# A hybrid attention trunk: difference heads divided by their sums as a row, and a short feed-forward with gate operands made step by step and up-projection in 512 columns

## The chip, the cores and the metric

The kernel runs on one core of a Trainium2 chip. The metric is the device time of one execution in microseconds (us), the median of several runs; lower is better. The core has five engines with instruction queues of their own: TensorE (PE, matrix products; its weight loads are shown apart as PEld), VectorE (DVE), ScalarE (ACT), GpSimd (POOL) and SyncE (SP, which here only issues transfers). Products land in PSUM, other tiles lie in SBUF, and transfers to and from memory run beside all engines.

## The reference, cut to what matters

One layer is applied to two sequences with shared weights: a long one of 1024 positions and a short one of 512, each with 16 learned positions ahead of it. D_MODEL is 1024, a head has 64 columns, D_FF is 2816.

```python
n = rms_norm(x, g_mix);  qa, ka, va, qb, kb, vb = split(n @ w_in)
# group A: 8 query heads over 2 key heads, softmax, times va
# group B: 4 difference heads, each with two softmax maps
s = einsum('bqhcd,bkhcd->bhcqk', qblk, kb) * scale
p = softmax(s, axis=-1)
a = p[:, :, 0] - lam * p[:, :, 1]
ob = einsum('bhqk,bkhe->bqhe', a, vb)
ob = rms_norm(ob, g_subln) * (1.0 - lam_init)
x = x + concat([oa, ob]) @ w_out

n = rms_norm(x, g_ffn);  gate = n @ w_ff_gate
gate = pad[:, :-2]*conv_w[0] + pad[:, 1:-1]*conv_w[1] + pad[:, 2:]*conv_w[2] + conv_b
x = x + (gelu(gate) * (n @ w_ff_up)) @ w_ff_down
```

A last rms_norm follows, and the 16 positions are dropped. Where rms_norm is taken of a difference head, a common factor of a query's 128 values cancels but for the 1e-6 that is added to their mean square.

## The kernel before, in words

Products are kept near float32: an operand is split into a rounded high part (a cast on ACT, L114) and a low part (a subtraction, L115, on DVE or POOL), and a product is three matmuls, high by high, high by low, low by high (`mm3`, L121 to L123). `dense` (L126) does this for eight blocks of 128 rows, 24 matmuls into one PSUM bank. Weights come as a whole tile w_f by SP's queue and are split in SBUF (`load_weight`, L171).

The stages, with the time at which they run in the profiled execution: the projection of the short sequence (to about 150 us); the short attention beside the long projection (to about 510); the long attention (`attention`, L383) beside the short sequence's output projection and feed-forward (`conv_glu`, L748), to about 1325; the long output projection, beside the rest of the short feed-forward (to about 1450); the long feed-forward in two layers of a seven-product scheme on half blocks (to the end). Two parts that run beside each other are generators that `merge` (L1234) advances in a given ratio of the costs that they yield. This gives the order in which instructions are written down. A planner with a model of the engines then sets each engine's own order and hands out buffers: what is written down first goes first, and where it isn't ready by the model, something later takes its place. On the chip each engine keeps the order that was set.

A difference head (`diff_block`, L523) takes a block of queries in two or three columns of tiles (102 to 114 queries each): three blocks for each of the 4 long heads, two for each of the 4 short heads, 20 blocks in all with 56 columns. For each column `softmax` (L424) makes scores (L431, L432), moves them from PSUM with their maximum (L433, L436), and takes Exp with the sum over keys in `l` (L438). Nothing is divided: p0 stays as it is, and p1 is scaled by c = -lambda * l0 / l1 (L531) and added (L532), so that the result is l0 times the wanted difference. `weighted_v` (L445) transposes it block of keys by block of keys (L456), splits it (pt_hi, pt_lo) and multiplies it by the values into the PSUM tile "o" (L466 to L468), of which there is one; L480 is the last, for the remaining keys. Then ACT copies o (L541) and squares it (L543), one matmul with ones_v takes the mean square into "o" again (L545), and `rsqrt_newton` (L98) makes the factor for L551. Since o is l0 times too large, the 1e-6 has to be l0 squared times as large: for each column ACT makes a tile e, the square of l0 times a constant (L535), and a matmul of e by the diagonal matrix eps_d adds it to the mean square (L548).

The short feed-forward takes the 22 blocks of D_FF in groups of two. For each block there are two chunks of 256 positions (`centres`, L768): gate with 258 columns and its convolution (L782 to L787), GELU over the group (L790), then up, multiplied by the gate (L802) and split, the low part a_lo on POOL (L803); then `down` (L808) for eight blocks of columns at 512 positions, added to h on DVE (L814). Between the weights of the group that begins with block 12 and its `down`, `presplit` (L868) makes four sums and differences of quarters of the first two gate weight tiles, splits them and stores them in memory for the long feed-forward (L884 to L894). Its subtractions run on DVE, and it has two steps.

## Time and profile before

| | |
|---|---|
| median of 3 runs | 2126.57 us (2126.3 to 2130.99) |
| profiled execution | 2138.1 us, its span 2136.3 us |
| granted TensorE clock, mean | 0.982 |
| chain that ended last | PE 76%, DVE 12%, DMA 4%, ACT 3%, issue 3% |
| HBM read, written | 211.13 MB, 82.85 MB |
| transfers, mean busy share of the 16 engines (hardware queue) | 41.6% |

A profile is one execution as the hardware profiler took it, on one core. Matmuls are pipelined: a row shows when one started and a modelled end, and neighbours overlap, so that the distance from start to start is the price of one in a row of them. "Idle before, releaser" is the time that an engine stood still ahead of a group and whose signal ended it. A group's line number can be that of a helper; then the tile names tell it apart. In the stretches, each engine's busy time and its count of instructions stand in the order PE, PEld, DVE, ACT, POOL, then the granted clock, the share of the transfer engines and GB/s. The lists of waits give the waiting instruction, the one that it waited for, the us in total, how often, and the longest.

### The profile page before, as it was taken

What the parts mean: (1) busy time and instruction counts of PE and PEld (TensorE: products, weight loads), DVE (VectorE), ACT (ScalarE), POOL (GpSimd) and SP (SyncE); (2) the same over time, 40 slices, a digit from 0 to 9 for tenths busy, and PEclk for the clock granted to TensorE, in tenths of its full rate; (3) what the DMA queues carried; (4) which work ended last, traced back from release to release, by engine and by line L of the source; (5) the groups of instructions that cost most, each with busy time, mean ns of one, the idle gap of its engine ahead of it and who ended that gap; (6) DMA issues with size and microseconds to landing.
All of it is one profiled execution on the core that took longest, in us unless ns stands there. A gap on an engine that the chain in (4) does not pass through costs nothing.

```text
span 2136.3 us, 35264 instructions
## 1 busy us (share of the span) xinstructions
PE 2051.1 (96%) x12302; PEld 1833.1 (86%) x12302; DVE 1724.1 (81%) x3786; ACT 1156.8 (54%) x2253; POOL 582.7 (27%) x534
## 2 busy tenths in 40 slices
PE   6999999999999999999999999979999999999998
PEld 6988888997887999899989999978888777778877
DVE  6878889767879788888988885578878878869886
ACT  6635566544657556666666765345444444435454
POOL 4653233553112000000000000542444444330112
PEclk8999999999999999999999999998999999999999
DMA  7564335456621322223352224986232232247443
GB/s 252 178 198 133 118 110 170 153 182 226 206 84 55 105 75 70 70 85 114 103 188 77 93 88 145 300 256 229 101 109 89 97 115 84 94 166 258 119 126 126
DMA packets 164897, 296.30 MB, mean 139 GB/s; under 512 B 21456, under 2 KB 82672, under 8 KB 164208
## 3 DMA queue, kind: packets, MB, share of 16 engines
q1 hardware_dynamic: 162416, 287.76, 41.6%
q0 software_dynamic: 2304, 6.29, 0.8%
q8 instruction: 97, 1.59, 0.3%
q14 instruction: 80, 0.66, 0.1%
HBM read 211.13 MB, written 82.85 MB: 138 GB/s over the span
## 4 chain that ended last, share of the span: by engine, by line
PE 76%; DVE 12%; DMA 4%; ACT 3%; issue 3%; POOL 1%; SPq 1%; DVEq 0%; ACTq 0%; POOLq 0%
PE ps_mm L121 17%; PE ps_mm L123 17%; PE ps_mm L122 17%; PE ps_t L456 5%; PE ps_s L431 3%; PE ps_s L432 3%; PE ps_s L121 2%; PE ps_s L122 2%; PE ps_s L123 2%; PE ps_o L471 2%; PE ps_o L470 2%; DVE p L433 1%; DVE w_lo L115 1%; DMA m<-oT 1%; DVE acc L979 1%
## 5 line engine op out<-in xcount | busy, mean ns | idle before, releaser
L121 PE MATMUL ps_mm<-xhi,w_hi 128*128 128x258 f32 (+3 forms) x1264 | 383.4, 304 | 12.0 <-ACT xhi L114 3.7
L122 PE MATMUL ps_mm<-xlo,w_hi 128*128 128x258 f32 (+3 forms) x1264 | 379.0, 300 | 0.3 <-POOL xlo L115 0.3
L123 PE MATMUL ps_mm<-xhi,w_lo 128*128 128x258 f32 (+3 forms) x1264 | 377.2, 299 | 0.3 <-DVE w_lo L115 0.3
L433 DVE TENSOR_SCALAR_CACHE_REDUCE p<-ps_s 114x344 f32<-114x344 f32 (+4 forms) x562 | 257.6, 488 | 30.2 <-PE ps_s L432 19.1
L114 ACT CAST pt_hi<-ps_t 128x512 fp32r<-128x512 f32 (+6 forms) x360 | 169.3, 483 | 181.0 <-PE ps_t L456 155.2
L121 PEld LDWEIGHTS ps_mm<-xhi,w_hi 128*128 128x128 f32 x1264 | 240.0, 190 | 17.5 <-ACT xhi L114 5.4
L438 ACT ACTIVATE p<-p,nm 114x1040 f32<-114x1040 f32 (+5 forms) x212 | 214.8, 1013 | 72.8 <-DVE nm L436 71.8
L115 DVE TENSOR_TENSOR w_lo<-w_f,w_hi 128x1024 fp32r<-128x1024 f32 (+1 forms) x182 | 192.8, 1067 | 66.2 <-ACT w_hi L114 65.6
L122 PEld LDWEIGHTS ps_mm<-xlo,w_hi 128*128 128x128 f32 x1264 | 240.3, 190 | 1.9 <-POOL xlo L115 0.7
L123 PEld LDWEIGHTS ps_mm<-xhi,w_lo 128*128 128x128 f32 x1264 | 240.0, 190 | 1.2 <-DVE w_lo L115 0.5
L114 ACT CAST w_hi<-w_f 128x1024 fp32r<-128x1024 f32 (+1 forms) x199 | 167.6, 856 | 84.9 <-PE ps_mm L122 57.5
L115 DVE TENSOR_TENSOR pt_lo<-ps_t,pt_hi 128x512 fp32r<-128x512 f32 (+4 forms) x312 | 171.7, 561 | 43.7 <-ACT pt_hi L114 42.3
L115 POOL TENSOR_TENSOR a_lo<-gate,a_hi 128x256 fp32r<-128x256 f32 x44 | 43.3, 985 | 545.3 <-ACT a_hi L114 525.9
L431 PE MATMUL ps_s<-k,q 128*114 128x348 f32 (+4 forms) x552 | 183.6, 338 | 3.4 <-DVE p L433 3.2
L456 PE MATMUL ps_t<-ident,p 128*128 128x128 f32 (+7 forms) x1188 | 183.0, 270 | 1.0 <-DVE nm L436 0.5
L432 PE MATMUL ps_s<-k,q 128*114 128x348 f32 (+4 forms) x552 | 171.1, 315 | 0.0
L121 PE MATMUL ps_s<-xhi,w_hi 128*128 128x256 f32 (+4 forms) x480 | 148.7, 313 | 20.4 <-ACT xhi L234 8.2
L456 PEld LDWEIGHTS ps_t<-ident,p 128*128 128x128 f32 (+7 forms) x1188 | 140.4, 136 | 29.6 <-issue 6.8
L123 PE MATMUL ps_s<-xhi,w_lo 128*128 128x256 f32 (+4 forms) x480 | 147.4, 307 | 1.4 <-DMA w_lo<-wo 1.4
L122 PE MATMUL ps_s<-xlo,w_hi 128*128 128x256 f32 (+4 forms) x480 | 148.6, 310 | 0.0
L121 PE MATMUL ps_mm<-t_hi,w_hi 128*128 128x512 f32 (+2 forms) x368 | 144.6, 393 | 1.2 <-DVE v L934 1.2
L123 PE MATMUL ps_mm<-t_hi,w_lo 128*128 128x512 f32 (+2 forms) x368 | 144.4, 392 | 0.1
(275 smaller groups left out, 5309.4 us busy)
## 6 DMA issues: line engine op xcount, KB each, us to landing
w_f<-w_gate SPq DMA_DIRECT2D x46, 512.0 KB, 3.5
w_f<-w_up SPq DMA_DIRECT2D x44, 512.0 KB, 3.4
w_f<-w_in SPq DMA_DIRECT2D x36, 512.0 KB, 3.9
a_f<-act SPq DMA_DIRECT2D x62, 256.0 KB, 2.7
w_f<-w_down SPq DMA_DIRECT2D x22, 512.0 KB, 3.3
act<-a_t SPq DMA_DIRECT2D x44, 256.0 KB, 2.1
a<-w_down SPq DMA_DIRECT2D x40, 256.0 KB, 5.4
w_hi<-wo SPq DMA_DIRECT2D x36, 256.0 KB, 5.1
```

The lines of the kernel that those rows point to most:

```text
L114: return (nc.scalar.copy(hi, src).ins, (lo_engine or nc.vector).tensor_tensor(out=lo, in0=src, in1=hi.bitcast(F32), op=ALU.subtract).ins)
L115: (lo_engine or nc.vector).tensor_tensor(out=lo, in0=src, in1=hi.bitcast(F32), op=ALU.subtract).ins)
L121: nc.tensor.matmul(ps, lhsT=whi, rhs=xhi, start=start, stop=False)
L122: nc.tensor.matmul(ps, lhsT=whi, rhs=xlo, start=False, stop=False)
L123: return nc.tensor.matmul(ps, lhsT=wlo, rhs=xhi, start=False, stop=stop).ins
L431: nc.tensor.matmul(ps, lhsT=q[0], rhs=k[:, c0:c0 + cw], start=True, stop=False)
L432: nc.tensor.matmul(ps, lhsT=q[1], rhs=k[:, c0:c0 + cw], start=False, stop=True)
L433: nc.vector.tensor_scalar(out=p[:, c0:c0 + cw], in0=ps, scalar1=HD ** -0.5, scalar2=-3.0e38, op0=ALU.mult, op1=ALU.max, accum_out=mx[:, i: ...
L438: g.last_exp = nc.scalar.activation(p, p, AF.Exp, bias=nm, accum_out=l).ins
L456: nc.tensor.transpose(tps[:, c:c + M], p[:, k0:k0 + kw], g.ident[:M, :M])
L470: nc.tensor.matmul(o, lhsT=v[:, i, :], rhs=hi, start=i == 0, stop=False)
L471: nc.tensor.matmul(o, lhsT=v[:, i, :], rhs=lo, start=False, stop=False)
```

## The change

In the difference heads the sums l0 of a block's columns are written next to each other into one tile of four columns. After the first block of keys of `weighted_v`, DVE takes their reciprocal, PE transposes it into a "t" tile of PSUM, ACT copies it to SBUF and issues from its own queue a transfer of it to a row in memory. After the second block of keys, SP issues a transfer that reads the row into all 128 partitions (the tile `r_rows`, one buffer). When the values are done, ACT copies o as before, POOL multiplies the copy by the row, and ACT squares that. The tiles e, the matrix eps_d and their matmuls are gone, and the 1e-6 is added in `rsqrt_newton` as elsewhere.

In the feed-forward of the short sequence up runs over 512 positions at once; gate remains at two chunks. `presplit` is advanced by one step after each of the eight column blocks of `down`, its steps are six, its subtractions and its sum run on POOL, and the quarter tiles are kept in the order 1, 2, 0, 3.

```diff
-    def softmax(q, k, inverse=True):
+    def softmax(q, k, inverse=True, l=None):
...
-        l = sp.tile([P, 1], F32, name="l", tag="l")[:M]
+        if l is None:
+            l = sp.tile([P, 1], F32, name="l", tag="l")[:M]
...
+    rows = op.tile([P, 512], F32, name="r_rows", tag="r_rows", bufs=1)
...
-    def diff_block(qs, ks, v, cols):
-        pl, el = [], []
-        for c0, M in cols:
-            p0, l0, _ = softmax([x[:, c0:c0 + M] for x in qs[0]], ks[0], False)
+    def diff_block(qs, ks, v, cols, row):
+        nt, M, W = len(cols), cols[0][1], sum(m for _, m in cols)
+        pl = []
+        l0 = sp.tile([P, 4], F32, name="l0", tag="l0", bufs=2)[:M, :nt]
+        for i, (c0, _) in enumerate(cols):
+            p0 = softmax([x[:, c0:c0 + M] for x in qs[0]], ks[0], False, l0[:, i:i + 1])[0]
             p1, _, r1 = softmax([x[:, c0:c0 + M] for x in qs[1]], ks[1])
...
-            e = op.tile([P, P], F32, name="e", tag="e", bufs=6)[:M]
-            nc.scalar.activation(e, g.ones_d[:M], AF.Square, scale=l0)
-            el.append(e)
             pl.append(p0)
             yield 4 * n
-        o, W = yield from weighted_v(pl, v, True)
+        value = weighted_v(pl, v, True)
+        yield next(value)
+        nc.vector.reciprocal(out=l0, in_=l0)
+        ps = g.psum.tile(nt, M, "t")
+        nc.tensor.transpose(ps, l0, g.ident[:M, :M])
+        lt = sp.tile([4, P], F32, name="lt", tag="lt", bufs=1)[:nt, :M]
+        nc.scalar.copy(lt, ps)
+        nc.scalar.dma_start(out=row[:W].rearrange("(t p) -> t p", p=M), in_=lt)
+        yield next(value)
+        nc.sync.dma_start(out=rows[:, :W], in_=row[:W].unsqueeze(0).broadcast_to([P, W]))
+        o, W = yield from value
         ob = op.tile([P, 512], F32, name="o_b", tag="o")[:, :W]
         nc.scalar.copy(ob, o)
+        nc.gpsimd.tensor_tensor(out=ob, in0=ob, in1=rows[:, :W], op=ALU.mult)
...
-        nc.tensor.matmul(ms, lhsT=g.ones_v, rhs=sq, start=True, stop=False)
-        for e, (c0, M) in zip(el, cols):
-            c = c0 - cols[0][0]
-            nc.tensor.matmul(ms[:, c:c + M], lhsT=e, rhs=g.eps_d[:M, :M], start=False, stop=e is el[-1])
+        nc.tensor.matmul(ms, lhsT=g.ones_v, rhs=sq, start=True, stop=True)
...
-        rsqrt_newton(g, op, rs, ms, W, 0.0)
+        rsqrt_newton(g, op, rs, ms, W)
...
-            for c0, cw in centres:
+            for c0, cw in even_chunks(N, 512):
                 up = g.psum.tile(P, cw, "mm")
...
-        if f0 == FPRE:
-            yield from presplit(g, wp, ap)
         if grp[-1] < NFF - 1:
+            pre = presplit(g, wp, ap) if f0 == FPRE else iter(())
             for j in range(KT):
                 for c0, cw in even_chunks(N, 512):
                     down(j, c0, cw)
                     yield 3 * len(grp) * cw
+                next(pre, None)
+            drain(pre)
             continue
...
     def minus(out, a, b):
-        nc.vector.tensor_tensor(out=out, in0=a, in1=b, op=ALU.subtract)
-
-    kept(0, raw[0])
+        nc.gpsimd.tensor_tensor(out=out, in0=a, in1=b, op=ALU.subtract)
+
     t = ap.tile([P, 2, H], F32, name="gate", tag="gate", bufs=1)
-    nc.vector.tensor_tensor(out=t[:, 0], in0=a21, in1=a22, op=ALU.add)
+    nc.gpsimd.tensor_tensor(out=t[:, 0], in0=a21, in1=a22, op=ALU.add)
     minus(t[:, 1], t[:, 0], a11)
+    yield
     kept(1, t.rearrange("p x c -> p (x c)"))
-    yield 0
+    yield
 
     minus(t[:, 1], a12, t[:, 1])
     minus(t[:, 0], a11, a21)
+    yield
     kept(2, t.rearrange("p x c -> p (x c)"))
+    yield
+    kept(0, raw[0])
+    yield
     kept(3, a22, H)
-    yield 0
```

The remaining edits give the function's callers the row (`g.r`, twelve rows in memory for each sequence) and take eps_d out of the constants.

More of the change, by code (lines that the diff above doesn't have):

```diff
@@ L561, in attention @@
         v = load_v(1 + h, 2 * P, 0)
-        rows = g.oT[s][512 + h * P:512 + (h + 1) * P]
+        out = g.oT[s][512 + h * P:512 + (h + 1) * P]
         for blk in blocks:
@@ L566, in attention @@
             qs = [load_q(QB + h, m, c0, W) for m in range(2)]
-            ob = yield from diff_block(qs, ks, v, [(c - c0, m) for c, m in blk])
+            ob = yield from diff_block(qs, ks, v, [(c - c0, m) for c, m in blk], g.r[s][h * len(blocks) + blocks.index(blk)])
             lead = 1 if c0 < NMETA else 0
             c1 = c0 + lead - (NMETA - 1)
-            nc.sync.dma_start(out=rows[:, c1:c1 + W - lead], in_=ob[:, lead:])
+            nc.sync.dma_start(out=out[:, c1:c1 + W - lead], in_=ob[:, lead:])
     if s == 1:
@@ L1275, in trunk_kernel @@
     dram = ctx.enter_context(tc.tile_pool(name="dram", bufs=1, space=DRAM))
-    g.qk, g.v, g.vt, g.oT = [], [], [], []
+    g.qk, g.v, g.vt, g.oT, g.r = [], [], [], [], []
     for s, N in enumerate(SEQS):
@@ L1283, in trunk_kernel @@
         g.oT.append(dram.tile([D, N + 1], F32, name=f"oT{s}"))
+        g.r.append([dram.tile([512], F32, name=f"rb{s}_{i}") for i in range(12)])
     g.h = dram.tile([KT, P, SEQS[0]], F32, name="h0")
@@ L1309, in trunk_kernel @@
     nc.vector.memset(g.eps, EPS)
-    g.eps_d = const.tile([P, P], F32, name="eps_d")
-    nc.vector.tensor_scalar(out=g.eps_d, in0=g.ident, scalar1=EPS * D * D, scalar2=None, op0=ALU.mult)
     g.gain = const.tile([P, V_CW], F32, name="gain")
```

3 lines of the change are left out of this document (2 added, 1 removed).

## Prediction

> **What bounds the kernel now.** I read the page first (busy shares), then busy time in the four stretches that hold what is edited, then who waited for whom on TensorE in them, and last the order of time around the edited lines.
>
> ```profile
> span 2136.3 us, 35264 instructions
> PE 2051.1 (96%) x12302; PEld 1833.1 (86%) x12302; DVE 1724.1 (81%) x3786; ACT 1156.8 (54%) x2253; POOL 582.7 (27%) x534
> ...
> core 0: us, PE busy (x) PEld busy (x) DVE busy (x) ACT busy (x) POOL busy (x), PEclk, DMA share, GB/s
> 300.00:500.00 200.00, 194.63 (x1297) 185.83 (x1297) 150.44 (x451) 106.38 (x269) 89.44 (x73) 1.00 0.49 157
> 975.00:1080.00 105.00, 105.00 (x770) 101.86 (x769) 93.75 (x273) 71.88 (x135) 6.80 (x7) 1.00 0.35 110
> 1080.00:1125.00 45.00, 40.94 (x242) 36.62 (x242) 39.27 (x101) 27.80 (x53) 0.74 (x1) 0.92 0.55 192
> 1125.00:1312.00 187.00, 186.68 (x1324) 177.34 (x1322) 154.56 (x408) 119.98 (x225) 12.61 (x12) 1.00 0.31 102
> ```
>
> The columns after the stretch are PE, weight loads, DVE, ACT, POOL, the granted clock. Stretch 300 to 500 holds the short sequence's difference heads beside the long projection; 975 to 1312 the long sequence's difference heads beside the short feed-forward; 1080 to 1125 the making of the gate operands. Outside 1080 to 1125 PE is busy for 486.3 of 492 us, while DVE has 93.3 us of idle time (49.6, 11.3 and 32.4) and ACT 193.8. So time falls where PE instructions fall away. What PE waits for in the last two stretches:
>
> ```profile
> PE ps_mm L121 <- DVE gate L802: 0.3, 1, 0.3
> ...
> PE ps_o L545 <- ACT o_sq L543: 3.1, 1, 3.1
> ...
> ACT w_hi L114 <- DMA w_f<-w_up: 3.0, 1, 3.0
> ...
> 1112.00:1120.00 8.00, 4.91 (x23) 4.24 (x22) 5.76 (x14) 7.27 (x16) 0.00 (x0) 0.72 0.40 127
> ```
>
> The first row is all that PE waits for from 1125 to 1300. The other three belong to the one hole of this stage: at 1112 ACT stands 3.0 us in front of a weight load that has not landed, the Square of a difference head is queued behind it on ACT, PE waits 3.1 us for that Square, and then goes on at a granted clock of 0.72.
>
> **Part 1: the sums leave PE as eps matmuls and come back as a row.** Removed are 56 tiles e on ACT and their matmuls.
>
> ```profile
> L548 PE MATMUL ps_o<-eps_d,e x112: 252/275/421, 352.8 to 1315.8; 114*128 114x114 f32 x72, 102*128 102x102 f32 x24, 104*128 104x104 f32 x16
> ...
> 1212.22 0.74 PE L545 MATMUL ps_o<-o_sq,ones_v 128*128 128x342 f32 x2
> 1212.80 0.82 PE L548 MATMUL ps_o<-eps_d,e 114*128 114x114 f32 x6
> 1213.39 0.36 PE L122 MATMUL ps_mm<-xlo,w_hi 128*128 128x256 f32 x1
> 1213.59 0.28 PE L123 MATMUL ps_mm<-xhi,w_lo 128*128 128x256 f32 x1
> 1213.71 0.46 PE L456 MATMUL ps_t<-ident,p 114*128 114x114 f32 x3
> 1213.93 0.36 PE L121 MATMUL ps_mm<-xhi,w_hi 128*128 128x256 f32 x1
> ...
> L535 ACT ACTIVATE e<-ones_d,l x56: 384/392/407, 304.0 to 1273.0; 114x128 f32<-114x128 f32 x36, 102x128 f32<-102x128 f32 x12, 104x128 f32<-104x128 f32 x8
> ...
> L584 POOL TENSOR_TENSOR acc<-acc,sq 128x342 f32<-128x342 f32 x7 | 7.0, 1003 | 2.0 <-ACT sq L583 2.0
> ```
>
> Durations overlap on PE, so the price is the distance of starts: six L548 take 1213.39 - 1212.80 = 0.59 us, and the matmul after them takes 0.20 instead of the 0.12 of its neighbours, together 0.67, or 0.112 each. 112 of them: 12.5 us. If the 0.08 behind them isn't theirs, 11.0. Added are 20 transposes of the sums, one for each block of a head. Three transposes take 0.22 plus the same 0.08, so 0.10 each and 2.0 us in all (3.0 if each brings that 0.08 alone: 20 x (0.07 + 0.08)). Net on PE -10.5 us, between -8.0 and -10.5. PE is short of time in 300 to 500 and 975 to 1312, so I count all of it.
>
> Off PE: ACT loses 56 x 0.392 = 22.0 us, and gains 20 copies of a few rows and 20 DMA issues, nothing that its 193.8 us of idle time doesn't take. DVE gains 20 reciprocals of a few columns. POOL gains 20 products of 128x342 or less, about 1.0 us each, 20 us where it was busy for 89 of 200 and 20 of 337. The tail of a block, which holds the one PSUM bank "o", becomes longer by that 1.0 and a hand-over, and shorter by 0.67: about +0.5 us for each block. PE covers that with projection or feed-forward matmuls. Uncovered it is 10 us.
>
> The new waits hang on the row's way through memory: ACT issues a small write, SP issues a read to 128 partitions.
>
> ```profile
> L521 SPq DMA_DIRECT2D oT<-o_a x16: 488/592/597, 258.7 to 970.6; - x16
> DMA to landing us min/median/max: 1.7/1.9/4.4
> ...
> L421 SPq DMA_DIRECT2D v_tail<-vt x12: 323/543/987, 154.6 to 1146.3; - x12
> DMA to landing us min/median/max: 1.7/3.8/6.9
> ...
> 428.81 0.26 PE L466 MATMUL ps_o<-pt_hi,v 128*128 128x208 f32 x1
> 433.91 0.34 PE L480 MATMUL ps_o<-pt_hi,v_tail 96*128 96x208 f32 x1
> ...
> 1225.59 0.32 PE L466 MATMUL ps_o<-pt_hi,v 128*128 128x342 f32 x1
> 1234.77 0.32 PE L480 MATMUL ps_o<-pt_hi,v_tail 96*128 96x342 f32 x1
> ```
>
> With the nearest small write and the nearest small read the trip is 1.9 + 3.8 us, two issues of 0.5 and about 0.5 for reciprocal, transpose and copy: 7.2 us; at the worst landings 12.8, at the best 4.9. From a block's second L466 (the first row of each pair) to its L480, the time that the trip has, these rows show 9.2 us for a long block and 5.1 for the smallest short one. So the long blocks are covered, the four smallest short ones may be 2 us late, and I book 0 for it, since projection matmuls stand between; the bounds are 0 and 8 us. Behind these waits stand: on SP the loads of q, k and weights, while the read waits 1.9 us for its row; on POOL the rotary sums (short heads) and the low parts a_lo (long heads); on ACT, behind the Square, the casts of pt_hi and the exponentials.
>
> **Part 2: up-projection in 512 columns.** 44 groups of 24 matmuls of 256 columns become 22 groups of 512: 528 pairs become 528 matmuls.
>
> ```profile
> 1311.88 0.28 PE L121 MATMUL ps_mm<-xhi,w_hi 128*128 128x256 f32 x1
> ...
> 1313.20 0.32 PE L480 MATMUL ps_o<-pt_hi,v_tail 96*128 96x342 f32 x1
> ...
> 714.81 0.39 PE L122 MATMUL ps_mm<-a_lo,w_hi 128*128 128x512 f32 x1
> ...
> 717.37 0.32 PE L431 MATMUL ps_s<-k,q 128*128 128x348 f32 x1
> ...
> L802 DVE TENSOR_TENSOR gate<-ps_mm,gate x44: 399/419/425, 690.2 to 1341.0; 128x256 f32<-128x256 f32 x44
> ...
> L814 DVE TENSOR_TENSOR h<-ps_mm,h 128x512 f32<-128x512 f32 x80 | 54.0, 685 | 11.9 <-PE ps_mm L123 11.0
> L115 POOL TENSOR_TENSOR a_lo<-gate,a_hi 128x256 fp32r<-128x256 f32 x44 | 43.3, 985 | 545.3 <-ACT a_hi L114 525.9 <-issue 16.4 <-ACT pt_hi L114 2.9
> L1032 POOL TENSOR_TENSOR a_t<-act 128x512 f32<-128x512 f32 x22 | 28.8, 1310 | 27.3 <-DMA act<-act 22.4 <-DVE act L1024 4.9
> ```
>
> Eleven matmuls of 256 stand between 1311.88 and 1313.20, 0.120 us each; eleven of 512 between 714.81 and 717.37, 0.2327 each. A pair costs 0.240, so 7.3 ns go with each pair: 528 x 7.3 ns = 3.8 us (2.2 to 5.4, as the starts are rounded to 0.01 us). The durations themselves (0.28 and 0.39) would promise 0.17 us for each pair, 90 us in all, but they overlap and are no price. DVE gains 22 x (2 x 0.419 - 0.685) = 3.4 us, POOL 22 x (2 x 0.985 - 1.31) = 14.5 us, which pays most of part 1's products. The last matmuls of a group wait longer for their operand, by about 0.27 on DVE and 0.3 on POOL; attention's matmuls cover it, 22 x 0.6 = 13 us if not.
>
> The Trainium skill (TensorE: Matmul & The Clock Gate, Back-to-back issue gap) gives N/2.4 + 2.5 ns for a warm matmul, so by it a pair would lose only the fixed 2.5 ns and the term would be 1.3 us. The trace's 120 and 232.7 ns lie above the page's 109 and 216, and I keep the trace's difference.
>
> **Part 3: gate operands step by step.** Four subtractions of 128x512 leave DVE (2.7 us at 0.683 each, L814's shape) for POOL (5.2 us at 1.31). The splits and the eight stores remain, in another order, spread over the eight column steps of the down-projection. In 1080 to 1125 PE is idle for 4.1 us and slowed after it: 0.72 of the clock for the PE busy 4.91 us of the quoted window is some 1.4 us more. The hole's start is a late weight load on ACT, and the raw weights now keep their two buffers as long as before or longer (kept(0) is made fourth). So I count the relief of DVE alone, 2.7 us, rounded to 3; bounds are 5.5 gained and 3 lost (one more such ACT wait).
>
> **Sum.** -10.5 - 3.8 - 3 = -17.3 us. The profiled execution took 2138.1 us with a span of 2136.3; it would come to 2120.8. The median of the runs is 2126.57, 11.5 us below that execution, and takes the same difference: 2109. The terms' own bounds (8.0 to 10.5, 2.2 to 5.4, -3 to 5.5) give 2105 to 2119.
>
> **Rivals.** *Late row.* The row lands after the values are ready. POOL stands before its product, ACT before the Square, and PE soon before pt_hi. It turns the sign once a block idles PE for over 17.3 / 20 = 0.87 us, and is measurably slower from 1.2 us. Had every block the 2.0 us of the smallest: +40 - 17.3, so 2149. Against it speak the 9.2 us of the long blocks and the other stream's matmuls; for it the landings of up to 6.9 and the in-order queues, as at 1112.
>
> *POOL holds DVE up.* One row pair bears on it:
>
> ```profile
> 425.19 1.57 DVE L551 SCALAR_TENSOR_TENSOR o_b<-o_b,gsub,o_rs 128x306 f32<-128x306 f32 x1
> ...
> 465.66 0.54 DVE L551 SCALAR_TENSOR_TENSOR o_b<-o_b,gsub,o_rs 128x306 f32<-128x306 f32 x1
> ...
> 424.04 2.39 POOL L115 TENSOR_TENSOR w_lo<-w_f,w_hi 128x1024 fp32r<-128x1024 f32 x1
> ```
>
> The first L551 began under the POOL instruction that ran to 426.43 and ended after it; the same shape takes 0.54 at 465.66. The new POOL work can hold DVE for 20 x 1.0 + 4 x 1.31 = 25.2 us (the 14.5 that part 2 takes off POOL left aside). Less the 6.1 that parts 2 and 3 spare DVE, 19.1 are left. If three quarters of that stand in PE's way, it is -17.3 + 14.3 = -3: 2124, no difference. The 93 us of DVE idle time speak against it. The Trainium skill (SBUF — State Buffer, SBUF: two separate sides) says that DVE operations with two SBUF inputs and POOL take turns on a port pair, the loser blocked for the whole instruction; by that rule this rival is the one to watch, and the row above agrees.
>
> *More goes.* The hole at 1112 closes wholly (5.5 instead of 3), and ACT's 22 us lighter load closes as much again in the other holes of 300 to 500, where PE lacks 5.4 us: -17.3 - 2.5 - 5.4 = -25, 2101.
>
> *It does less than it says*: matmuls of 512 columns at twice the price of 256; then 3.8 us are missing, 2113, inside the forecast.
>
> **Numbers.** What a measurement of this kernel can tell from no change is 0.3%, 6.4 us: faster is below 2120, slower above 2133. Forecast 0.60, more goes 0.20, POOL holds DVE up 0.13, late row 0.07. So faster 0.80, same 0.13, slower 0.07. The range reaches from below the third rival, 2096 (5 us for a schedule that is made anew), to 2124 of the second; the late row is left out.
>
> **What would show it.** L548 and L535 gone; on PE 528 up-projection matmuls at 0.233 us from start to start; PE busy falling by some 14 us in 300 to 500 and 975 to 1312 together, with those stretches shorter by as much. Part 3 is right if the hole of 3 us behind 1105 is smaller and the clock stays at 1.00. The forecast is wrong if PE waits for the Square or for pt_hi in every block, if POOL is shown waiting for rows by more than a microsecond a block, or if new holes appear at 500 to 545 and 1350 to 1450, where stages change over.

## The result, and the profile after

The kernel after takes 2154.57 us, median of 4 runs (2153.7 to 2156.8); the one before took 2128.78 beside it (2126.3 to 2131.22). The ratio is 1.0121 [1.0107, 1.0135]: slower by 26 us, where 17 us faster was forecast. The profiled execution took 2156.8 us with a span of 2155.0, 18.7 more than the span before. The traces thus hold 19 of the 26 us: the profiled execution before was itself 9 us above its median.

The page of the kernel after:

```profile
span 2155.0 us, 34065 instructions
PE 2054.1 (95%) x11682; PEld 1800.9 (84%) x11682; DVE 1732.5 (80%) x3779; ACT 1142.2 (53%) x2195; POOL 599.3 (28%) x536
```

TensorE has 620 matmuls fewer, as foreseen (112 and 528 gone, 20 new), and yet 3 us more of busy time. Its busy time is no measure of work here: a modelled duration is also longer where the next matmul starts later (one of 512 columns shows 0.47 us where the next starts 0.31 us behind it, and 0.39 where it starts 0.23 behind). The same stretches as in the prediction, and two more (the columns are PE, weight loads, DVE, ACT, POOL, granted clock, share of the transfer engines, GB/s):

```profile
300.00:500.00 200.00, 192.51 (x1249) 181.68 (x1248) 153.54 (x456) 101.68 (x256) 94.08 (x80) 0.98 0.51 161
975.00:1080.00 105.00, 102.62 (x612) 91.27 (x610) 88.63 (x248) 63.39 (x112) 15.35 (x10) 1.00 0.42 135
1080.00:1125.00 45.00, 43.78 (x272) 39.42 (x272) 38.80 (x108) 30.93 (x56) 5.65 (x4) 1.00 0.52 172
1125.00:1312.00 187.00, 186.19 (x1186) 169.63 (x1185) 165.09 (x464) 122.10 (x218) 15.42 (x12) 1.00 0.25 78
1300.00:1340.00 40.00, 30.15 (x190) 24.46 (x189) 22.65 (x63) 19.29 (x44) 2.75 (x3) 0.93 0.38 124
...
1338.00:1464.00 126.00, 107.84 (x598) 101.91 (x599) 81.62 (x135) 51.52 (x108) 57.77 (x76) 0.91 0.87 271
```

The heads' stretches, whose busy time was to fall by some 14 us, have 192.51 (194.63 before), 102.62 (105.00) and 186.19 (186.68). That is 5 us less busy time in stretches of the same length: TensorE stands idle for these 5 us and is not through sooner. The hole of 1080 to 1125 has shrunk (43.78 busy of 45, was 40.94, clock 1.00). New is the one of 1300 to 1340: 9.9 us idle, clock 0.93. The kernel before had there

```profile
1300.00:1340.00 40.00, 39.07 (x288) 38.41 (x287) 19.80 (x49) 20.75 (x38) 5.58 (x7) 1.00 0.52 136
```

What TensorE waits for there in the kernel after, at the end of the long attention:

```profile
PE ps_s L121 <- ACT xhi L114: 2.6, 1, 2.6
PE ps_o L558 <- ACT o_sq L556: 2.0, 1, 2.0
PE ps_o L467 <- DVE o_rs L106: 2.0, 1, 2.0
PE ps_t L457 <- DVE pt_lo L115: 1.5, 3, 0.8
PE ps_o L481 <- ACT pt_hi L479: 1.1, 2, 0.8
```

The first is the long output projection itself, which waits for the split of the last head's output; the others are links of a difference head's own chain. Every block has these links, before and after, and in most of them feed-forward matmuls run beside the links. In the kernel after the last feed-forward matmul of this stretch starts at 1314.2, and none runs from there to the projection at 1338.8. The long output projection behind it (the last stretch) has lost its cover too: 107.84 busy of 126, where the kernel before had

```profile
1319.00:1446.00 127.00, 114.25 (x727) 110.49 (x726) 84.00 (x151) 52.72 (x112) 59.14 (x80) 0.96 0.86 262
```

The clock falls too, from 0.96 to 0.91. The Trainium skill (TensorE: Matmul & The Clock Gate, Why this matters for your kernels) asks for no gaps over about 3 us between bursts of matmuls. The traces show that the longest gap does not decide alone: the clock is 0.93 at 1300 where no listed wait is longer than 2.6 us, and in the projection the kernel before has the longer single wait (8.5 us for h, 5.3 after) and the higher clock.

**An account.** For each shape of matmul I take the median distance to the next start over the whole trace, and call what a distance has beyond that idle (a shorter distance counts as negative). So "idle" is all that is not matmul time at the usual distance, a lower clock included. Three stretches are cut at 510 us and at the first matmul of the long output projection; the third lasts to the projection's last matmul. "Left" is the feed-forward matmuls, at their usual distance, that run after the projection has begun. "Query group" is the last value matmul of the eight long query heads, a stage in which the heads' part of the change does not occur. Times are us of each kernel's one profiled execution; the ratio is of the runs, to the kernel before on the same chip.

| kernel | ratio, 95% | query group | left | projection begins | idle to 510 | idle 510 to projection | idle in it | its length |
|---|---|---|---|---|---|---|---|---|
| before | | 967 | 16.2 | 1319.7 | 64.7 | 48.0 | 18.6 | 126.3 |
| after | 1.0121 [1.0107, 1.0135] | 997 | 1.4 | 1338.8 | 72.5 | 59.1 | 31.9 | 124.7 |
| e1 heads | 0.9987 [0.9971, 1.0003] | 964 | 2.9 | 1316.8 | 70.1 | 38.6 | 27.5 | 121.8 |
| e2 wide up | 1.0053 [1.0036, 1.0070] | 991 | 1.4 | 1330.9 | 64.8 | 48.6 | 30.5 | 123.3 |
| e3 gate steps | 1.0011 [0.9993, 1.0029] | 964 | 20.0 | 1308.9 | 65.9 | 41.1 | 17.4 | 129.0 |
| e4 after, two groups held | 1.0123 [1.0090, 1.0156] | 992 | 10.5 | 1333.9 | 70.5 | 64.9 | 25.8 | 127.8 |
| e5 after, paced | 1.0096 [1.0081, 1.0111] | 967 | 10.5 | 1332.0 | 70.9 | 62.6 | 24.2 | 126.0 |
| e6 e5, product on DVE | 1.0048 [1.0033, 1.0063] | 966 | 10.0 | 1326.6 | 67.8 | 60.0 | 21.0 | 122.3 |
| e7 e10, product on DVE | 0.9962 [0.9947, 0.9977] | 961 | 9.3 | 1312.6 | 66.3 | 44.0 | 19.2 | 119.8 |
| e8 wide, evicted in halves | 1.0107 [1.0090, 1.0123] | 996 | 1.4 | 1341.0 | 65.3 | 57.3 | 28.4 | 121.4 |
| e9 narrow, one bank | 1.0008 [0.9997, 1.0020] | 970 | 6.4 | 1324.6 | 66.1 | 43.3 | 19.4 | 117.4 |
| e10 heads and gate steps | 1.0044 [1.0028, 1.0059] | 970 | 1.4 | 1330.5 | 72.7 | 47.2 | 26.6 | 119.8 |
| e11 after, product on DVE | 1.0088 [1.0070, 1.0106] | 993 | 1.4 | 1334.0 | 66.5 | 59.2 | 25.3 | 118.3 |
| e12 e7, one bank | 1.0015 [1.0004, 1.0026] | 969 | 11.1 | 1315.6 | 67.9 | 47.2 | 25.0 | 127.6 |
| e13 before, narrow down | 1.0047 [1.0032, 1.0063] | 967 | 11.1 | 1322.8 | 65.6 | 46.8 | 21.8 | 124.3 |
| e14 e7, narrow down | 1.0001 [0.9991, 1.0011] | 966 | 10.6 | 1317.2 | 69.2 | 47.9 | 22.6 | 124.6 |
| e15 e7, mean in bank t | 1.0164 [1.0145, 1.0183] | 971 | 1.4 | 1347.9 | 75.7 | 63.0 | 28.4 | 121.4 |
| e16 e1, product on DVE | 0.9996 [0.9985, 1.0008] | 962 | 3.6 | 1313.3 | 67.0 | 38.7 | 25.8 | 120.9 |
| e17 e7, last group late | 1.0031 [1.0019, 1.0042] | 963 | 29.4 | 1301.4 | 67.4 | 51.9 | 24.9 | 145.7 |
| e18 e7, last two late | 1.0069 [1.0055, 1.0083] | 966 | 46.9 | 1294.4 | 68.1 | 61.6 | 22.6 | 160.8 |

What follows the projection takes 687 to 693 us in every kernel. For the kernel after, the start of the projection moves by -14.3 (the matmul time that the prediction took away, 10.5 + 3.8) + 14.8 (feed-forward work that used to run later) + 7.8 + 11.1 (idle) = 19.4 us; the trace has 19.1. Done the same way, the account meets the start of the projection within 2.1 us in all the other kernels but e13 and e14, which it puts 6 us late. Since idle is defined as the rest, this confirms the matmul time that was counted, and not a cause of the idle time. Over the whole span, with the 12.4 and 14.3 us that lie behind the projection, TensorE's idle time goes from 143.7 to 177.8 us, +34.1, against the 14.3 saved: +19.8, where the spans differ by 18.7. So the saving is there, and it was given back more than twice over as idle time. Of the 13.3 us that the projection idles longer, some 5 would be the clock's alone (an estimate: 9% of 107.84 us less 4% of 114.25).

That missing cover is what makes attention idle can be read from all twenty traces. I cut the time from 510 us to the projection into pieces of 25 us, counted back from the projection, 640 in all. Where feed-forward matmuls are at least 0.4 of a piece's matmul time, TensorE idles for 0.7 us on average (567 pieces); between 0.2 and 0.4 for 6.3 (49 pieces), and below 0.2 for 7.6 (24 pieces). In all, the pieces below 0.4 hold 19.7 us of idle time in the kernel before and 34.6 in the kernel after, the other pieces 22.0 and 22.9. In the last piece before the projection the share is 0.74 and the idle time 0.9 us in the kernel before, 0.03 and 13.7 us in the kernel after.

### The profile page after: what moved, and what is told of

It reads as the page before. It is cut to its first block, busy times and chain, and to the rows that moved or that the text cites. A ratio compares the mean times of both kernels' runs of the same rounds, so it can differ in the third digit from the quotient of the medians.

```text
span 2155.0 us, 34065 instructions
## 1 busy us (share of the span) xinstructions
PE 2054.1 (95%) x11682; PEld 1800.9 (84%) x11682; DVE 1732.5 (80%) x3779; ACT 1142.2 (53%) x2195; POOL 599.3 (28%) x536
## 5 line engine op out<-in xcount | busy, mean ns | idle before, releaser
L121 PE MATMUL ps_mm<-xhi,w_hi 128*128 128x258 f32 (+4 forms) x1088 | 355.2, 327 | 8.6 <-ACT xhi L114 4.0
L122 PE MATMUL ps_mm<-xlo,w_hi 128*128 128x258 f32 (+4 forms) x1088 | 351.4, 323 | 0.4 <-POOL xlo L115 0.3
L123 PE MATMUL ps_mm<-xhi,w_lo 128*128 128x258 f32 (+4 forms) x1088 | 349.9, 322 | 0.3 <-DVE w_lo L115 0.3
L433 DVE TENSOR_SCALAR_CACHE_REDUCE p<-ps_s 114x344 f32<-114x344 f32 (+4 forms) x562 | 258.7, 488 | 36.0 <-PE ps_s L432 26.6
L121 PEld LDWEIGHTS ps_mm<-xhi,w_hi 128*128 128x128 f32 x1088 | 208.1, 191 | 20.2 <-ACT xhi L114 6.4
L122 PEld LDWEIGHTS ps_mm<-xlo,w_hi 128*128 128x128 f32 x1088 | 208.1, 191 | 8.9 <-POOL xlo L115 0.7
L123 PEld LDWEIGHTS ps_mm<-xhi,w_lo 128*128 128x128 f32 x1088 | 207.7, 191 | 8.4 <-DVE w_lo L115 0.8
L122 PE MATMUL ps_mm<-t_lo,w_hi 128*128 128x512 f32 (+2 forms) x368 | 144.5, 393 | 0.0
```

What stands on the lines that cost most here:

```text
L121: nc.tensor.matmul(ps, lhsT=whi, rhs=xhi, start=start, stop=False)
L122: nc.tensor.matmul(ps, lhsT=whi, rhs=xlo, start=False, stop=False)
L123: return nc.tensor.matmul(ps, lhsT=wlo, rhs=xhi, start=False, stop=stop).ins
L433: nc.vector.tensor_scalar(out=p[:, c0:c0 + cw], in0=ps, scalar1=HD ** -0.5, scalar2=-3.0e38, op0=ALU.mult, op1=ALU.max, accum_out=mx[:, i: ...
```

## The experiments

**The three parts alone.** e1 has the heads' hunks, e2 the wide up-projection, e3 the gate steps.

```diff
# e2: the kernel before with
-            for c0, cw in centres:
+            for c0, cw in even_chunks(N, 512):
                 up = g.psum.tile(P, cw, "mm")
```

> The difference heads' part alone, feed-forward and gate operands as before. Theory 'balance' (wider up-projection matmuls let the short feed-forward run ahead, so that attention's last heads and the start of the long output projection stand without cover): most of the loss is missing here; the 10 us of PE work that go are nearly used up by a smaller loss of cover, 2120 to 2132, ratio 0.995 to 1.003. Theory 'tail' (POOL product and row make each difference head longer): the loss is all here, 2145 to 2160, ratio 1.008 or more.

> The up-projection in 512 columns alone. Balance: the feed-forward's last group is through before the last difference heads, PE idle 10 us or more between 1290 and 1345, time 2138 to 2150, ratio 1.005 to 1.011. Tail: nothing of the loss is here, 3.8 us of PE work go, 2122 to 2127, ratio 0.997 to 1.000.

> The gate operands step by step alone. Balance and tail both: 2 to 8 us faster, 2120 to 2126, the hole at 1112 smaller. If late gate weights are the loss: slower than before, 2135 or more.

Measured 0.9987, 1.0053 and 1.0011. Alone, none does what it was booked for, and together they are worse (1.0121) than their product (1.0051). The heads save 10.5 us of matmuls and gain 3, which their interval does not tell from nothing. In the account 5.4 come back as idle time in the short heads, 9.4 go between 510 and the projection, and 13.3 are feed-forward work that now lies ahead of the projection, whose idle time grows by 8.9. The wide up-projection, booked at -3.8 us, costs 11. The gate steps miss the 2 to 8 us that were expected of them.

**Holding the feed-forward back.** My first theory was that the feed-forward has run ahead of attention, the query group ends 30 us later (997, was 967) with the matmuls used up early, and so the last difference heads stand uncovered. e4 holds the gate matmuls of the last two groups behind values of the long attention, e5 all groups from the third, so that each has about the place that it had before.

```diff
# e4, e5: the kernel after with
-            dense(g, gp, wg[f], xhi, xlo, c0, cw + 2)
+            with behind(g, *([g.done[0][HOLD[f0]]] if f0 in HOLD else [])):
+                dense(g, gp, wg[f], xhi, xlo, c0, cw + 2)
+HOLD = {18: 26, 20: 28}    # e4: first block of a group: value matmul that it waits for
+HOLD = {4: 10, 6: 13, 8: 15, 10: 18, 12: 20, 14: 22, 16: 24, 18: 26, 20: 28}    # e5
```

> The changed kernel with all its parts, and the gate matmuls of the feed-forward's last two groups placed behind the value matmuls of the ninth and eleventh long difference block, so that work is left to cover the last heads. Balance: most of the loss comes back, 2115 to 2132, ratio 0.994 to 1.002, and the hole after 1300 closes. Tail: holding work back cannot help, 2150 or more, ratio 1.010 or more.

> The changed kernel with all its parts; from the third group on, the feed-forward's gate matmuls stand behind the value matmuls of a given attention block (the 11th for the third group, then every second or third, the 29th for the last), so that the feed-forward is used up as slowly as in the kernel before, from the query-group heads on. The run before this one, held at the last two groups only, moved the hole from after 1300 to 1200-1250 and won nothing. Balance: with even pacing no stretch of 50 us between 1000 and 1350 has a hole of over 8 us, and the time is 2115 to 2136, ratio 0.995 to 1.004. If attention's own length is what costs: 2145 or more, ratio 1.008 or more.

Measured 1.0123 and 1.0096. In e5 the query group ends at 967 as before, and 10.5 us are left for the projection, yet the idle time from 510 to the projection is 62.6 us (after 59.1, before 48.0): the hole moved and was not filled. So running ahead is not the whole cause. In e5 the pieces of 25 us with a share below 0.4 idle for no longer than before (20.0 us), but all others for 33.6 us instead of 22.0: the two streams cover each other worse even where both are there. The holding itself may be part of that, since no kernel with the narrow up-projection was paced in this way.

**The heads' tail.** In e6, e7 and e11, and later in e16, DVE multiplies the values by the row straight from PSUM, in the place of ACT's copy and POOL's product.

```diff
-        nc.scalar.copy(ob, o)
-        nc.gpsimd.tensor_tensor(out=ob, in0=ob, in1=rows[:, :W], op=ALU.mult)
+        nc.vector.tensor_tensor(out=ob, in0=o, in1=rows[:, :W], op=ALU.mult)
```

> As the paced kernel, and DVE makes the product with the row straight from PSUM in place of ACT's copy and POOL's product, so that a difference head's tail is about 1 us shorter. Balance with even pacing: no more than 3 us faster than the paced kernel, since PE sets the time there. Tail: 10 us or more faster than the paced kernel (12 us for 12 long blocks).

> The heads' part with the product made by DVE straight from PSUM, and the gate operands step by step; up-projection in 256 columns as before. Balance: feed-forward work lasts to the last block, the PE work that goes (10.5 us) shows, 2112 to 2126, ratio 0.993 to 0.999. Tail: the same, as the tail is short again. Neither, if the heads' PE work is not what the time is made of: 2128 or more.

> Parts 1 and 3 of the change as they stand (copy of the values on ACT, product on POOL), up-projection at 256 columns. Theory 'tail' (the product on POOL behind a copy on ACT lengthens the time in which the one bank of values is held): it is 4 to 6 us slower than the same kernel with the product on DVE straight from PSUM, so ratio 0.9975 to 0.9995. Rival: the gain of that kernel is the gate steps together with the heads and the place of the product is worth nothing here: ratio 0.995 to 0.997.

> The whole change, only that DVE multiplies the values by the row straight from PSUM; the copy on ACT and the product on POOL are gone. Theory 'tail' worth 5 us by itself and the run-ahead of the feed-forward another matter: ratio 1.006 to 1.010, the feed-forward as far ahead as in the change (last query-group values near 990 us). Rival (the long tail is what makes attention fall behind, so the run-ahead goes with it): ratio 1.000 to 1.004, last query-group values near 967.

In pairs that differ in nothing else: e5 to e6 1.0096 to 1.0048, after to e11 1.0121 to 1.0088, e10 to e7 1.0044 to 0.9962, so 10, 7 and 17 us gained. e10, slower than the kernel before, lies outside both ranges that were expected of it. Part of the gain shows in the last value matmul of the last six short blocks, in the kernel before, after, and e11:

```profile
L480 PE MATMUL ps_o<-pt_hi,v_tail x6: 263/365/407, 390.0 to 493.6; 96*128 96x208 f32 x3, 96*128 96x306 f32 x3
```
```profile
L481 PE MATMUL ps_o<-pt_hi,v_tail x6: 258/324/409, 390.6 to 497.5; 96*128 96x208 f32 x3, 96*128 96x306 f32 x3
```
```profile
L481 PE MATMUL ps_o<-pt_hi,v_tail x6: 258/283/409, 390.7 to 491.8; 96*128 96x208 f32 x3, 96*128 96x306 f32 x3
```

Five blocks take 103.6, 106.9 and 101.1 us. One block's chain in the kernel after:

```profile
441.29 0.30 ACT L553 COPY o_b<-ps_o 128x208 f32<-128x208 f32 x1
...
442.84 0.37 ACT L556 ACTIVATE o_sq<-o_b 128x208 f32<-128x208 f32 x1
...
446.89 0.42 ACT L103 ACTIVATE rs_y<-ps_o,eps 128x208 f32<-128x208 f32 x1
...
451.53 0.43 DVE L106 SCALAR_TENSOR_TENSOR o_rs<-ps_o,eps,o_rs 128x208 f32<-128x208 f32 x1
```
```profile
L554 POOL TENSOR_TENSOR o_b<-o_b,r_rows x2: 636/738/841, 441.7 to 465.6; 128x208 f32<-128x208 f32 x1, 128x306 f32<-128x306 f32 x1
...
L561 DVE SCALAR_TENSOR_TENSOR o_b<-o_b,gsub,o_rs x1: 1209/1209/1209, 454.1 to 454.1; 128x208 f32<-128x208 f32 x1
```

From the copy to the Square it is 1.55 us: POOL begins at 441.7 and takes 0.64, and the Square is behind it. In the kernel before it came at once:

```profile
L541 ACT COPY o_b<-ps_o x2: 332/374/415, 434.3 to 455.3; 128x208 f32<-128x208 f32 x1, 128x306 f32<-128x306 f32 x1
...
L543 ACT ACTIVATE o_sq<-o_b x2: 379/426/474, 434.8 to 455.8; 128x208 f32<-128x208 f32 x1, 128x306 f32<-128x306 f32 x1
```

In the kernel after, the bank is free only when L106 has read it, 10.7 us after the copy's start, and the last step, L561, comes at 454.1. The gain is no law, though: with the heads alone it was nothing, e1 to e16 0.9987 to 0.9996 (-2 us, within the intervals), although there too the idle time to 510 falls, from 70.1 to 67.0.

> Part 1 alone with the product on DVE straight from PSUM; presplit as before, up in 256 columns. If the gate steps are worth the 2.7 us of DVE that I counted: ratio 0.996 to 0.999, 1 to 3 us slower than with them. Rival (the gate steps cost as much as they give): 0.993 to 0.9965.

e16 lies above both ranges that were expected of it. It was meant to price the gate steps as well, and with e3 it leaves them open: added to before they cost 2 us (e3, within its interval of -1.5 to 6.2), added to e1 12 (e10), and taken from e7 they are missed by 7 (e16).

**What is wide about the wide up-projection.** e8 keeps the wide matmuls and multiplies, casts and splits in halves as before; e9 keeps the narrow matmuls and does the rest over 512 columns from one bank.

```diff
# e8: the kernel before with
-            for c0, cw in centres:
-                up = g.psum.tile(P, cw, "mm")
-                dense(g, up, wu, xhi, xlo, c0 + 1, cw)
+            up = g.psum.tile(P, N, "mm")
+            dense(g, up, wu, xhi, xlo, 1, N)
+            for c0, cw in centres:
# e9: the kernel before with
-            for c0, cw in centres:
+            for c0, cw in even_chunks(N, 512):
                 up = g.psum.tile(P, cw, "mm")
-                dense(g, up, wu, xhi, xlo, c0 + 1, cw)
+                for d0, dw in centres:
+                    dense(g, up[:, d0:d0 + dw], wu, xhi, xlo, d0 + 1, dw)
```

> The kernel before with the up-projection's matmuls in 512 columns, but multiplied by the gate and split in two halves of 256 as before, so that only the matmuls' width differs. If the width itself (a filler that takes PE for twice as long each time it is let in) makes the feed-forward run ahead: as the wide one alone or slower, 2138 to 2155, ratio 1.004 or more. If the fewer and longer operations on DVE, ACT and POOL do: as before, 2122 to 2131, ratio 0.997 to 1.002.

> The kernel before with one edit: both chunks of 256 positions of an up-projection go into one PSUM bank of 512 columns, by 256-column matmuls as before; product, cast and low part are taken over 512 columns at once. So the matmuls are narrow and the bank and what follows it are as in the change. Theory 'width' (the 512-column matmul itself delays attention's next ready matmul): ratio 0.997 to 1.001, last query-group values near 967 us, last GELU near 1316. Rival 'bank' (one bank that takes twice the work lets the feed-forward run ahead, whatever the width of its matmuls): ratio 1.005 to 1.011 like the two kernels with wide matmuls, last query-group values at 990 us or later, last GELU at 1291 or earlier.

Measured 1.0107 and 1.0008. The same PSUM bank, and 21 us between them. e8 from 510 on, then e9:

```profile
510.00:1341.00 831.00, 807.45 (x4970) 710.23 (x4969) 693.50 (x1896) 512.29 (x926) 76.27 (x86) 0.99 0.33 105
1341.00:1463.00 122.00, 103.00 (x601) 95.97 (x600) 80.08 (x132) 50.24 (x106) 56.78 (x76) 0.96 0.88 276
```
```profile
510.00:1324.00 814.00, 800.52 (x5457) 728.50 (x5457) 690.82 (x1869) 512.07 (x905) 65.43 (x65) 1.00 0.33 107
1324.00:1442.00 118.00, 107.48 (x645) 102.10 (x644) 83.81 (x142) 50.60 (x106) 56.23 (x76) 0.96 0.90 284
```

In the first of each pair PE stands still for 23.6 us (831 less 807.45) and 13.5, in the second for 19.0 and 10.5. So it is neither the longer wait for an operand of 512 columns nor the fewer evictions. It is the matmuls' width: three pairs differ in next to nothing else, before to e8 +23 us (the same halves, but in one bank), e9 to e2 +10 and e12 to e11 +16 (the same bank and the same evictions). In the four pairs where the eviction changes as well it is before to e2 +11 us, e9 to e8 +21, e10 to after +16, e7 to e11 +27. In the five kernels with wide up-projection and no holding in that stage (after, e2, e4, e8, e11) the query group ends at 991 to 997, in the thirteen with the narrow one at 961 to 971.

**Is it width as such?** If a stream's share of TensorE went with the width of its matmuls, narrow ones in the down-projection would let the feed-forward fall back. e12 tries the one bank on e7, e13 and e14 the narrow down-projection on before and on e7.

```diff
# e13, e14
-            for i, ((ahi, alo), (dhi, dlo)) in enumerate(zip(acts, wd)):
-                mm3(g, ps, dhi[:, j * P:(j + 1) * P], dlo[:, j * P:(j + 1) * P],
-                    ahi[:, c0:c0 + cw], alo[:, c0:c0 + cw], i == 0, i == len(acts) - 1)
+            for d0, dw in even_chunks(cw, 256):
+                for i, ((ahi, alo), (dhi, dlo)) in enumerate(zip(acts, wd)):
+                    mm3(g, ps[:, d0:d0 + dw], dhi[:, j * P:(j + 1) * P], dlo[:, j * P:(j + 1) * P],
+                        ahi[:, c0 + d0:c0 + d0 + dw], alo[:, c0 + d0:c0 + d0 + dw], i == 0, i == len(acts) - 1)
```

> The fastest kernel so far (parts 1 and 3, product on DVE from PSUM, narrow up-projection matmuls) with both chunks of an up-projection in one bank and one product of 512 columns. Theory 'width': 0.994 to 0.997, the fewer evictions gaining up to 3 us or nothing. Rival 'bank': 1.001 or more, the feed-forward ahead by 25 us at the end of the query group.

> The kernel before, up in 256 columns as it was, but the down-projection's matmuls of 512 columns are made as two of 256 into the same bank (528 become 1056, 7.3 ns of TensorE more for each pair, 3.9 us). Theory 'width' (the share of TensorE that the feed-forward gets beside attention grows with the columns of its matmuls): the feed-forward falls back, the query group's last values come before 967 us (950 to 960), more than 16 us of feed-forward matmuls are left when the long output projection begins, last GELU after 1316 us; ratio 0.994 to 1.000. Rival (the order is made anew by any edit and the shift has nothing to do with width): the shift goes either way, ratio 1.000 to 1.006.

> The fastest kernel so far (heads and gate steps, product on DVE straight from PSUM, up in 256 columns), with the down-projection in matmuls of 256 columns too. Theory 'width': more feed-forward work left for the long output projection than the 9.3 us of that kernel (15 us or more), ratio 0.992 to 0.997. Rival as in the run before: 0.997 to 1.004.

Measured 1.0015, 1.0047 and 1.0001. The query group does not come earlier (967 in e13, as before; 966 in e14, for 961 in e7), and what is left for the projection falls to 11.1 us in e13 (before 16.2) and is 10.6 in e14 (e7 9.3), not the 15 and more that were expected. The theory falls as a rule: wide up matmuls shift the streams, narrow down matmuls don't shift them back. And e12 loses 11 us on e7 by an edit that cost before nothing that its interval shows.

**Two tries to use what was learnt.** e15 takes the mean square into a bank of the transposes, so that the bank of the values is free once DVE has multiplied them.

```diff
-        ms = g.psum.tile(P, W, "o")
+        ms = g.psum.tile(P, W, "t")
```

> The fastest kernel so far, with the mean square of a difference head in a bank of the transposes (tag t) and not in the bank of the values, so that the next block's values can begin as soon as DVE has multiplied the last ones. Theory 'tail' (the one bank of values, held for 9 to 11 us after the last value matmul, is what spaces the blocks): short blocks 2 to 4 us closer, long blocks as before or closer, ratio 0.990 to 0.995. Rival (the bank isn't what spaces them, or the transposes now wait for the mean): ratio 0.996 to 1.003.

Measured 1.0164. The casts of the transposes, in e15 and then in e7 from 1080 to 1312:

```profile
ACT pt_hi L114 <- PE ps_t L457: 36.1, 22, 3.3
```
```profile
ACT pt_hi L114 <- PE ps_t L457: 18.3, 14, 4.0
```

ACT waits twice as long for the transposes, which now share their two banks with the mean. That the bank of the values spaces the blocks was not borne out, and the loss lies above both ranges that were expected. That the two banks of the transposes are the scarcer is not shown: TensorE is as busy in that stretch as in e7 (228.42 and 228.62 of 232 us). The idle time is longer by 9.4 us up to 510 and by 19.0 from there to the projection, for which 1.4 us of feed-forward work are left.

e17 and e18 let the last group, or the last two, wait for the end of the long attention, since the projection had seemed to take 117 to 129 us whatever ran beside it.

```diff
# as e4, on e7
+HOLD = {20: 29}            # e17
+HOLD = {18: 28, 20: 29}    # e18
```

> The fastest kernel so far, only that the gate matmuls of the last feed-forward group wait for the last value matmul of the long attention; its up and down follow them. About 22 us more of feed-forward matmuls are then left when the long output projection begins (31 us, where that kernel has 9.3). Account (work beside the output projection is mostly free: its length goes with a quarter of what rides beside it): the projection begins 22 us earlier less some 9 us that the last difference block idles without cover, and takes 5 us longer: 8 us faster than that kernel, ratio 0.991 to 0.995. Rival (the work isn't free there, or attention idles for as long as it is taken away): 0.9965 to 1.003.

> The same with the last two groups: the gate matmuls of the last but one wait for the values of the long attention's last but one block, those of the last group for its last block. About 39 us more are left for the output projection than in the fastest kernel. Account: 39 us less ahead of it, two to three difference blocks without cover at 9 us each (18 to 27 us), the projection longer by 10 us: about as fast as that kernel, ratio 0.994 to 0.999. Rival: slower than that kernel by 10 us or more, 1.001 to 1.008.

Measured 1.0031 and 1.0069. e17 and e18, from 510 and in the projection:

```profile
510.00:1301.00 791.00, 771.48 (x5190) 700.19 (x5189) 677.67 (x1872) 490.42 (x871) 72.86 (x86) 0.99 0.35 111
1301.00:1447.00 146.00, 128.58 (x835) 124.27 (x834) 89.84 (x162) 61.01 (x121) 59.18 (x79) 0.95 0.77 236
```
```profile
510.00:1294.00 784.00, 759.69 (x5096) 685.98 (x5095) 670.63 (x1870) 489.17 (x870) 71.57 (x84) 0.99 0.35 110
1294.00:1455.00 161.00, 143.12 (x934) 138.22 (x933) 98.46 (x172) 64.16 (x123) 63.84 (x81) 0.95 0.72 224
```

The projection begins 11 and 18 us earlier than e7's 1312.6, and lasts 26 and 41 us longer, for 20 and 38 us of added matmuls. By these lengths only some ten microseconds of work fit into its gaps; what is pushed behind that is paid in full, and attention idles for 8 and 18 us more without it. The reading that work beside the projection is mostly free was wrong beyond those ten.

## Why the prediction was wrong

The signs of its terms were taken from TensorE's matmuls alone, and that count was right: at the median distances the matmul time falls from 1973.4 to 1959.3 us, by 14.1 where 14.3 was booked. What failed is the sentence "PE is short of time in 300 to 500 and 975 to 1312, so I count all of it", and the one it leans on, that projection or feed-forward matmuls cover whatever else the change lengthens. In their place the runs showed 34.1 us more of idle time. The cover is a second stream, of fixed size, in an order that is set when the kernel is built. An edit in either stream changed how they lie against each other, and the forecast allowed for that only 5 us of a schedule made anew, on the faster side.

**Part 1** was booked at -10.5 us with a tail of +0.5 a block covered, or "uncovered it is 10 us". Uncovered is what happened in the short heads: idle time to 510 rose by 5.4 us (e1) to 8.0 (e10), and taking the copy and POOL out of the chain brought most of it back (66.3 to 67.8 in e6, e7, e11 and e16, before 64.7). The rest was lost where the feed-forward had less left for the projection. Heads alone: -3 us [-6.2, 0.6].

**Part 2** was booked at -3.8 us, its waits at 13 us if attention did not cover them. It costs 10 to 27 us, and not by those waits: e8 and e9. Its price of 0.2327 us for a wide matmul holds (over the whole trace the medians are 0.233 and, for a narrow one, 0.119, which makes the saving 2.6 us). The step that failed is that its price on TensorE is its price. Why wide up matmuls let the query group fall 24 to 30 us behind is open. The order comes from the planner, and no trace shows why it set the order that it did; that a wide matmul is a longer thing to stand behind was tried in e13 and e14, and they speak against it as a rule.

**Part 3** was right in its place: the hole at 1112 is closed. From 1112 to 1120 the kernel after has

```profile
1112.00:1120.00 8.00, 8.00 (x44) 6.91 (x43) 4.46 (x11) 4.23 (x8) 2.98 (x2) 1.00 0.57 171
```

for the 4.91 of 8 at 0.72 before. As time it was booked at -3 and measured at +2 [-1.5, 6.2] alone; what it is worth is not settled.

**The rivals.** The late row is refuted. Its read and what waits for the product, over the kernel after:

```profile
L550 SPq DMA_DIRECT2D r_rows<-rb x20: 319/331/530, 340.1 to 1322.0; - x20
...
DMA to landing us min/median/max: 2.9/3.0/3.5
```
```profile
L554 POOL TENSOR_TENSOR o_b<-o_b,r_rows x20: 626/920/1733, 350.1 to 1333.3; 128x342 f32<-128x342 f32 x12, 128x208 f32<-128x208 f32 x4, 128x306 f32<-128x306 f32 x4
...
  ACT o_b L553: 170.0, 12
  DMA w_f<-w_down: 28.0, 1
  DVE pt_lo L115: 13.3, 1
  PE ps_t L457: 0.5, 1
...
  ACT o_sq L556: 7.8, 9
```

The trace tells the landing of five of the twenty reads: they land within 3.5 us, where 3.8 was booked and 6.9 allowed. The product begins 10.0 us or more behind the issue of its read in all twenty blocks, and among what ended POOL's idle time before it the row does not occur (it is ACT's copy, 12 times). In the last line, the Square waits 7.8 us for POOL in all. "POOL holds DVE up" named the right engine in part 1, but not, as far as the pairs show, the way in which it costs: the product lengthens the chain. The step L561 took 1.23 us twice between 440 and 500, at 0.54 before for the larger of the two shapes:

```profile
L561 DVE SCALAR_TENSOR_TENSOR o_b<-o_b,gsub,o_rs x2: 1209/1232/1256, 454.1 to 474.1; 128x208 f32<-128x208 f32 x1, 128x306 f32<-128x306 f32 x1
...
452.66 2.43 POOL L115 TENSOR_TENSOR w_lo<-w_f,w_hi 128x1024 fp32r<-128x1024 f32 x1
```

The one at 454.1 began under the POOL instruction that ran to 455.09, as the Trainium skill (SBUF — State Buffer, SBUF: two separate sides) would have it; but that is a weight's low part, which was there before. In e11, with no product on POOL, the same step still took up to 2.31 us. Up to 1320 us, what DVE's instructions take beyond the quickest of the same shape (the median of the quickest quarter) is 68 us in the kernel before, 74 in the kernel after and 73 in e11, 76 in e10 and 75 in e7. With the product gone from POOL, DVE gets back 1 or 2 us of the 7 and 17 that these two pairs gain, so it is not DVE's being held up that carries the loss. None of the rivals was a shift between the streams, and the range's upper end of 2124 left out what happened. Its own list of signs had "new holes" at 500 to 545 and 1350 to 1450, "where stages change over"; they came at 1300 to 1340 and in the projection.

The kernel that beats both is e7: parts 1 and 3 with the product on DVE from PSUM and the up-projection as it was, 2122.76 us, 0.9962 [0.9947, 0.9977]. Its edge is 8 us, less than an edit that adds no work moved the same kernel (e12, 11 us), so a good deal of it may be the luck of an order.

## What to carry to other kernels

Where two streams are laid over each other by a planner, matmul time taken out of one need not be time won: write down TensorE's idle time by stage and the work that each stage leaves for the next, before and after, and forecast those. Expect such a kernel to move by 10 us or more either way for an edit that changes next to no work, give the forecast that width, and test an edit alone and with the others. Try a product that stands between the last matmul and the release of its bank on the engine that reads PSUM itself: here it gained in three pairs and nothing in a fourth.

## What the runs showed of the hardware

- A row of up to 342 floats sent through memory and read into 128 partitions landed in 2.9 to 3.5 us in the five of twenty cases whose landing the trace of the kernel after tells; the nearest small reads, which the prediction went by, took 3.8 in the median and 6.9 at most.
- Halving the columns of the down matmuls (480 were halved; the expectation counted 528) was costed at 3.9 us and cannot be found: the account with that price is 6 us too late in e13 and e14 alike. Two narrow ones in a row are 117 ns apart there in the median, so a pair takes 234 ns where the wide one took 233.
- Executions of the kernel before spread from 2123.8 to 2135.0 us on one chip, so that two profiled executions may differ by 10 us with nothing changed.
